# Split weights kept in DRAM, queries split at the projection, constants loaded one stage earlier, and 32-row scan blocks copied by ScalarE

## The chip, the cores and the metric

The kernel runs on one core of a Trainium2 chip. The metric is the device time of one execution in microseconds. The core has a matrix engine (PE, with its weight loads shown as PEld), a vector engine (DVE), an activation engine (ACT), a general engine (POOL), a queue engine (SP) that does nothing but issue transfers, and 16 DMA engines that carry the transfers of all queues. Each engine runs its own instruction list strictly in order; semaphores make one wait for another. An instruction that waits therefore holds everything behind it on its engine, and for SP that means every transfer behind a waiting one.

## What is computed

Two layers of an encoder over 2048 tokens of width 1024. Each layer normalises its input, multiplies it with one wide input matrix, feeds three head groups (A: gated linear attention, B: softmax attention with the difference of two maps, C: a gated recurrence), gates each group, multiplies with an output matrix, normalises and adds:

```python
for layer in range(2):
    h = rms_norm(x, norm_pre[layer])
    proj = h @ w_in[layer]                       # 1024 x 4128
    (gq, gk, gv, gg, gaf, gab, dq, dk, dv, dg, hq, hzf, hzb, hi, hg) = split(proj)
    y_a = gla_branch(gq, gk, gv, gg, ...)        # two scans, forward and backward
    y_b = diff_branch(dq, dk, dv, dg, ...)       # rope(q), rope(k), softmax(q1 k1) - lam softmax(q2 k2)
    y_c = hgrn_branch(hq, hzf, hzb, hi, hg, lb)  # f = lb + (1-lb) sigmoid(z); two scans
    x = x + rms_norm(concat(y_a, y_b, y_c) @ w_out[layer], norm_post[layer])
```

Accuracy is kept by splitting a float32 number into a rounded high part and the rest: a product of two split matrices is three matrix products (high by high, high by low, low by high).

## The kernel before, in words

Each layer has four stages. **Part 0** projects tokens 0 to 1023, block by block: 16 blocks of 256 (once 288) columns of the input matrix. **Part 1** projects tokens 1024 to 2047 with the same 16 blocks, and between the projection's matmuls the scans of groups A and C are worked off. **Attention** sweeps 64 units (4 heads by 16 query blocks), and the **output stage** multiplies, normalises and adds. The blocks come in the order of two lists in the code: values, gates, keys and queries of A and C first, then values of B, two blocks of keys (`do_qk(..., "k", ...)`), two blocks of queries (`do_qk(..., "q", ...)`) and three blocks of gates.

A block's weights come through `wload_into`: in two halves POOL's queue loads raw float32 (`wraw`, one buffer), DVE casts the high part (`whi`), and the rest (`wlo`) is subtracted by POOL in part 0 and by DVE in part 1. `whi` and `wlo` have two buffers, so that the next block's weights are made while this block is multiplied. Part 1 loads and splits every block's weights again.

`do_qk` works in groups of 512 tokens, two in each part: 48 matmuls fill two PSUM banks, DVE makes four products with a table of cosines and sines (`cs`, one buffer, loaded for each group by SP), POOL adds them into `ru`. A key is then split (`rh` cast by ACT, `ru` minus `rh` by POOL) and stored to `dr_k`; a query is stored whole to `dr_q`. Keys and queries of four heads lie 32 rows each in DRAM, so that one store of 128 rows by 512 columns has the outer sizes 4 and 32:

```python
nc.sync.dma_start(dr_q[hc, half, :, sl], u)   # hc: 4 of 8 heads, 32 rows each
```

In attention `load_q` brings the queries of two blocks back in four transfers, and POOL splits them. `layer_constants` loads two small sets of vectors and a small matrix at the start of a layer, in the middle of the first blocks. `do_hz` makes the gates of group C: DVE copies the projection out of PSUM, ACT and DVE work out the logarithm and exponentials, and POOL (part 0) or DVE (part 1) scales by `oml`. In the scans, `put` moves the blocks of levels 3 to 6 out of PSUM by a masked copy on DVE (L613), and those of level 7 by two plain copies of 64 rows on ACT.

PSUM has eight banks. In part 0 the projection may use all eight; in part 1 it has four, and the scans have the other four. The order of instructions on each engine is set when the program is built, by a scheduler with a model of costs; on the chip it is fixed. The small working tiles of the projection (`ru`, `rz`, `rh`, `z`, `lse`, `lsm`, `vs`, ...) share one set of seven buffers (tag `t`), and a tile that is stored is held until its store has landed.

Of the kernel before, what the change touches and what calls it, by code (L numbers as in the profile page):

```python
# [11 lines left out]
F32 = mybir.dt.float32  # L12
# [9 lines left out]
P = 128  # L22
# [38 lines left out]
def tile_hybrid_encoder(  # L61
# [40 lines left out]
    dr_q = dram.tile([8, 2, 32, L], F32, name="dr_q")  # L102
# [8 lines left out]
    dr_x = dram.tile([L, D], F32, name="dr_x")  # L111
    dr_u = dram.tile([P, 16, 512], F32, name="dr_u")
# [95 lines left out]
    def wload_into(wp, l, eng, c0, n, halves=False):  # L208
        hi = wp.tile([P, KC, WN], F32R, tag="whi", name="whi")
        lo = wp.tile([P, KC, WN], F32R, tag="wlo", name="wlo")  # L210
        for q in range(2):
# [3 lines left out]
            if halves:  # L215
                for hf in range(2):
                    src = raw[:, :, :n].rearrange("p k (h s i) -> p k h s i", s=2, i=32)[:, :, :, hf]
                    dh = hi[:, ks, P * hf:P * hf + P].rearrange("p k (h i) -> p k h i", i=32)
                    dl = lo[:, ks, P * hf:P * hf + P].rearrange("p k (h i) -> p k h i", i=32)
                    nc.vector.tensor_copy(dh, src)  # L220
                    eng.tensor_tensor(dl, src, dh.bitcast(F32), op=ALU.subtract)
            else:
                nc.vector.tensor_copy(hi[:, ks, :n], raw[:, :, :n])
                eng.tensor_tensor(lo[:, ks, :n], raw[:, :, :n], hi[:, ks, :n].bitcast(F32), op=ALU.subtract)  # L224
# [14 lines left out]

    for l in range(DEPTH):  # L240
# [6 lines left out]
        ls = lay.tile([P, 2], F32, tag="ls", name="ls")  # L247
        neglam = lay.tile([P, 1], F32, tag="neglam", name="neglam")
        wa2 = lay.tile([96, 2, P], F32R, tag="wa2", name="wa2")
        ba = lay.tile([P, 2], F32, tag="ba", name="ba")  # L250
# [5 lines left out]
        with ExitStack() as s1:  # L256
# [11 lines left out]
            def layer_constants():  # L268
                lv = ev.tile([P, 512], F32, tag="t", name="lv").rearrange("p (a n) -> p a n", n=64)
                lp = ev.tile([P, 512], F32, tag="t", name="lp").rearrange("p (a n) -> p a n", n=64)[:, :2]  # L270
                for i, a in enumerate((diff_lq1, diff_lk1, diff_lq2, diff_lk2)):
                    nc.sync.dma_start(lv[:, i], a[l:l + 1].to_broadcast([P, 64]))
                for i in range(2):
                    nc.vector.tensor_tensor(lp[:, i], lv[:, 2 * i], lv[:, 2 * i + 1], op=ALU.mult)
                nc.vector.reduce_sum(ls, lp, axis=AX.X)
                nc.scalar.activation(ls, ls, AF.Exp)
                nc.vector.tensor_tensor(neglam, ls[:, 1:2], ls[:, 0:1], op=ALU.subtract)
                nc.vector.tensor_scalar(neglam, neglam, -lam_init, None, op0=ALU.add)

                wraw = ev.tile([96, 512], F32, tag="t", name="wa").rearrange("p (d n) -> p d n", d=4)[:, :2]  # L280
                nc.vector.memset(wraw, 0.0)
                for d, (wa, b) in enumerate(((gla_wa2_fwd, gla_ba_fwd), (gla_wa2_bwd, gla_ba_bwd))):
                    for i in range(3):
                        nc.sync.dma_start(wraw[32 * i + 16 * d:32 * i + 16 * d + 16, d], wa[l])
                    nc.sync.dma_start(ba[:, d:d + 1], b[l].unsqueeze(1))
                nc.vector.tensor_copy(wa2, wraw)
                nc.vector.tensor_tensor(wa2[64:96], wraw[64:96], wa2[64:96].bitcast(F32), op=ALU.subtract)
# [36 lines left out]
            def do_qk(c0, cb, which, part):  # L324
                hc = slice(4 * cb, 4 * cb + 4)
                w = wload(c0 + 256 * cb, 256, part, halves=True)
                for g in (2 * part, 2 * part + 1):
# [5 lines left out]
                    for half, (a, b, op) in enumerate(((p1, p2, ALU.subtract), (p2, p1, ALU.add))):  # L333
# [4 lines left out]
                        nc.gpsimd.tensor_tensor(u, u, z, op=op)  # L338
                        if which == "q":
                            nc.sync.dma_start(dr_q[hc, half, :, sl], u)  # L340
                        else:
                            rh = ev.tile([P, 512], F32R, tag="t", name="rh")
                            nc.scalar.copy(rh, u)
                            nc.gpsimd.tensor_tensor(u, u, rh.bitcast(F32), op=ALU.subtract)
# [6 lines left out]
            def do_vs(c0, dst, dst0, part, w=None):  # L351
                w = w or wload(c0, 256, part)
# [81 lines left out]
            def do_hz(c0, d, part):  # L434
                w = wload(c0, 256, part)
                for m in range(2):
                    for g in (2 * part, 2 * part + 1):
                        ps = mm_ch(w, m * P, g)
                        sl = slice(g * 512, (g + 1) * 512)
                        z = ev.tile([P, 512], F32, tag="t", name="zh")  # L440
                        nc.vector.tensor_copy(z, ps)
                        e, lm = log_sig(z)
                        f = ev.tile([P, 512], F32, tag="t", name="f")
                        nc.scalar.activation(f, lm, AF.Exp)
                        he = nc.gpsimd if part == 0 else nc.vector
                        he.tensor_scalar(f, f, oml[:, l, m:m + 1], lb[:, l, m:m + 1], op0=ALU.mult, op1=ALU.add)
                        he.tensor_scalar(f, f, F_FLOOR, None, op0=ALU.max)
                        nc.sync.dma_start(dr_fh[d, m, :, sl], f)
                        kk = ev.tile([P, 512], F32, tag="t", name="kk")
                        nc.vector.scalar_tensor_tensor(e, z, 0.0, e, op0=ALU.max, op1=ALU.add)  # L450
                        nc.scalar.activation(kk, e, AF.Exp, scale=-1.0)
                        he.tensor_scalar(kk, kk, oml[:, l, m:m + 1], None, op0=ALU.mult)
# [27 lines left out]
            for i, b in enumerate(first + rest):  # L480
                b(0)
                if i == 0:
# [7 lines left out]
                    layer_constants()  # L490
# [9 lines left out]
            def scan_group(ti, g, tot):  # L500
# [91 lines left out]
                for lev in range(1, 8):  # L592
# [6 lines left out]
                    else:  # L599
# [5 lines left out]
                        def put(a, ps, j, lev=lev):  # L605
# [529 lines left out]
```

## Time and profile before

| | |
|---|---|
| median of 3 runs | 3637.28 us (3628.71 to 3641.9) |
| the profiled execution | 3641.44 us, of it span 3639.6 us |
| PE busy | 3513.4 us, 97% |
| DVE, ACT, POOL busy | 2560.3, 1927.8, 1459.6 us |
| DMA | 430.49 MB, mean 118 GB/s |

The profile is of one execution, whose time lies 0.1% above the median. "Busy" counts the time in which an engine had an instruction under way. Matmuls overlap one another, so PE counts as busy also where it runs slower than it could; a stretch of PE at the lower of its two clock levels (1.2 and 2.4 GHz) counts as busy too, and shows in the granted clock. Layer 0 takes about the first 1828 us and layer 1 the rest; the stages of layer 0 lie at 0 to 395 (part 0), 395 to 1003 (part 1, scans until about 920), 1003 to 1630 (attention) and 1630 to 1828 us (output).

### The profile page before, as it was taken

To read this page: it belongs to the slowest core of one execution; us is meant where nothing else is said; L and a number is where in the kernel's file an instruction comes from. 1 tells how busy PE (TensorE), PEld (TensorE's weight loads), DVE (VectorE), ACT (ScalarE), POOL (GpSimd) and SP (SyncE) were. 2 spreads that over 40 slices of the span, in tenths; PEclk is the share of its full clock that TensorE was granted. 3 is DMA by queue.
4 is the path that set the end of the run, shared out by engine and by line. 5 is a ranking of instruction groups with operands and counts; after the bars stand their busy time and mean duration, and the time that the engine had idled before them with its cause. 6 is when DMAs were issued, how large, how long until landed. Compare 5 with 4: busy or idle time off the path is not lost.

```text
span 3639.6 us, 62254 instructions
## 1 busy us (share of the span) xinstructions
PE 3513.4 (97%) x23296; PEld 3159.5 (87%) x23296; DVE 2560.3 (70%) x4426; ACT 1927.8 (53%) x4340; POOL 1459.6 (40%) x1454
## 2 busy tenths in 40 slices
PE   8999999998989999999989999999999899999999
PEld 7898988987978999888878989889878799999887
DVE  5422699987389999985324227999863899999733
ACT  4520455542377888874225215555423778888722
POOL 4545410012476667720035454100125867767100
PEclk9999999998999999999999999999989999999999
DMA  4444544544441333213334444445444413322143
GB/s 155 127 139 134 151 128 139 157 126 139 136 133 34 120 109 97 73 43 132 120 109 128 140 136 139 140 145 154 133 123 141 125 42 120 118 83 73 34 139 116
DMA packets 293645, 430.49 MB, mean 118 GB/s; under 512 B 42400, under 2 KB 185312, under 8 KB 291040
## 3 DMA queue, kind: packets, MB, share of 16 engines
q1 hardware_dynamic: 268896, 333.71, 29.7%
q0 software_dynamic: 22336, 90.71, 8.4%
q8 instruction: 184, 3.01, 0.3%
q10 hardware_dynamic: 2112, 2.10, 0.2%
q14 instruction: 117, 0.96, 0.1%
HBM read 275.82 MB, written 152.57 MB: 118 GB/s over the span
## 4 chain that ended last, share of the span: by engine, by line
PE 67%; DVE 13%; DMA 10%; POOL 4%; issue 3%; ACT 1%; SPq 1%; DVEq 0%; POOLq 0%; ACTq 0%
PE pp L306 14%; PE pp L297 12%; PE pob L1045 10%; PE po L938 9%; PE s L875 5%; PE s L876 5%; PE pt L927 5%; DMA wraw<-in_w_in_dram 3%; DVE mx L880 3%; DMA cs<-c_rope 2%; PE pm L587 2%; DVE e L921 2%; PE pm L568 1%; DMA ust<-dr_u 1%; PE poi L825 1%
## 5 line engine op out<-in xcount | busy, mean ns | idle before, releaser
L880 DVE TENSOR_REDUCE mx<-s 128x1 f32<-128x1024 f32 x512 | 623.1, 1217 | 54.3 <-PE s L876 52.9
L889 ACT ACTIVATE e<-s,mx 128x1024 f32<-128x1024 f32 x512 | 571.7, 1121 | 74.8 <-DVE mx L880 53.3
L306 PE MATMUL pp<-wlo,hhi 128*128 128x256 f32 (+1 forms) x2048 | 589.1, 288 | 7.1 <-POOL wlo L224 6.8
L306 PE MATMUL pp<-whi,hhi 128*128 128x256 f32 (+1 forms) x2048 | 585.2, 286 | 5.5 <-DVE ru L335 4.5
L306 PE MATMUL pp<-whi,hlo 128*128 128x256 f32 (+1 forms) x2048 | 588.4, 287 | 0.5 <-DVE hlo L195 0.5
L938 PEld LDWEIGHTS po<-vt,wt 128*128 128x128 f32 x4096 | 537.6, 192 | 47.9 <-ACT o L945 5.8
L938 PE MATMUL po<-vt,wt 128*128 128x128 f32 x4096 | 544.0, 276 | 1.6 <-ACT o L945 1.6
L875 PE MATMUL s<-ks,aqh 128*128 128x512 f32 x1024 | 452.4, 442 | 19.8 <-ACT e L889 15.1
L214 POOL DMA_DIRECT2D wraw<-in_w_in_dram x124 | 96.0, 774 | 920.4 <-DVE wlo L224 348.6
L876 PE MATMUL s<-ks,aql 128*128 128x512 f32 x1024 | 407.2, 398 | 14.2 <-POOL aql L732 14.1
L297 PE MATMUL pp<-hhi,whi 128*128 128x512 f32 x1024 | 412.5, 403 | 0.0
L297 PE MATMUL pp<-hlo,whi 128*128 128x512 f32 x1024 | 411.2, 402 | 0.0
L297 PE MATMUL pp<-hhi,wlo 128*128 128x512 f32 x1024 | 409.0, 399 | 0.0
L306 PEld LDWEIGHTS pp<-wlo,hhi 128*128 128x128 f32 x2048 | 390.0, 190 | 10.5 <-POOL wlo L224 7.6
L306 PEld LDWEIGHTS pp<-whi,hhi 128*128 128x128 f32 x2048 | 391.9, 191 | 8.0 <-issue 4.8
L921 DVE SCALAR_TENSOR_TENSOR e<-e,gam 128x1024 f32<-128x1024 f32 x256 | 392.3, 1533 | 0.0
L306 PEld LDWEIGHTS pp<-whi,hlo 128*128 128x128 f32 x2048 | 390.5, 191 | 1.8 <-DVE hlo L195 0.7
L931 ACT COPY wt<-pt 128x512 f32<-128x512 f32 x512 | 301.3, 589 | 118.9 <-PE pt L927 115.7
L927 PE MATMUL pt<-ident,e 128*128 128x128 f32 x2048 | 310.1, 274 | 1.2 <-ACT wt L931 0.6
L927 PEld LDWEIGHTS pt<-ident,e 128*128 128x128 f32 x2048 | 241.9, 142 | 2.9 <-ACT wt L931 1.2
L875 PEld LDWEIGHTS s<-ks,aqh 128*128 128x128 f32 x1024 | 196.4, 192 | 51.7 <-ACT e L889 23.3
L297 PEld LDWEIGHTS pp<-hhi,whi 128*128 128x128 f32 x1024 | 194.6, 190 | 45.0 <-issue 0.9
(190 smaller groups left out, 7042.9 us busy)
## 6 DMA issues: line engine op xcount, KB each, us to landing
wraw<-in_w_in_dram POOLq DMA_DIRECT2D x116, 512.0 KB, 4.8
cs<-c_rope SPq DMA_DIRECT2D x32, 512.0 KB
dr_gate<-z SPq DMA_DIRECT2D x64, 256.0 KB
aq<-dr_q SPq DMA_DIRECT2D x256, 64.0 KB
ks<-dr_k POOLq DMA_DIRECT2D x16, 1024.0 KB, 8.0
y<-dr_y SPq DMA_DIRECT2D x32, 512.0 KB
dr_qs<-qt SPq DMA_DIRECT2D x48, 256.0 KB
qs<-dr_qs SPq DMA_DIRECT2D x24, 512.0 KB
```

The lines of the kernel that those rows point to most:

```text
L214: nc.gpsimd.dma_start(raw[:, :, :n], w_in[l].rearrange("(k p) c -> p k c", p=P)[:, ks, c0:c0 + n])
L297: nc.tensor.matmul(ps.rearrange("p (a t) -> p a t", t=P), w[a][:, k, c:c + P], b[g][:, :, k], start=n == 0, stop=n == 3 * KC - 1)
L306: nc.tensor.matmul(ps, b[g][:, t % 4, k], w[a][:, k, :n], start=cnt == 0, stop=cnt == 3 * KC - 1)
L875: nc.tensor.matmul(s[:, i], self.qh[:, c, js], kk, start=True, stop=False)
L876: nc.tensor.matmul(s[:, i], self.ql[:, c, js], kk, start=False, stop=True)
L880: nc.vector.tensor_reduce(mx[:, k:k + 1], self.s[k].rearrange("p a n -> p (a n)"), axis=AX.X, op=ALU.max, negate=True)
L889: nc.scalar.activation(self.es[c][:, n * 1024:(n + 1) * 1024], self.s[kk].rearrange("p a n -> p (a n)"), AF.Exp, bias=self.mx[:, m:m + 1], ...
L921: nc.vector.scalar_tensor_tensor(es[0][:, hs], es[1][:, hs], gm[:, 8 + n:9 + n], es[0][:, hs], op0=ALU.mult, op1=ALU.add)
L927: nc.tensor.transpose(pt[:, i], self.es[0][:, (4 * q + i) * P:(4 * q + i + 1) * P], ident)
L931: nc.scalar.copy(wt, self.pt[q])
L938: nc.tensor.matmul(self.po, self.wt[q][:, i], self.v[:, k], start=k == 0, stop=k == NT - 1)
L1045: nc.tensor.matmul(pos[:, n], a[:, k], b[k][:, n * 512:(n + 1) * 512], start=cnt == 0, stop=cnt == 3 * KC - 1)
```

## The change

Four edits. (1) The split weights of part 0 are stored to DRAM (`dr_w`, by SP) and part 1 loads them ready made (`w_again`, POOL's queue, twice the bytes of the raw weights), with no cast and no subtraction. (2) A query is split in `do_qk` like a key, and each half is stored twice, in the layout in which attention wants it: eight stores for a group of 512 tokens instead of two. `load_q` is two transfers and no arithmetic. (3) `layer_constants` of layer 1 is issued at the start of layer 0's output stage. (4) In the scans the blocks of level 6 (32 rows by 32 columns) leave PSUM by four plain copies on ACT instead of one masked copy on DVE; and `do_hz` reads PSUM directly, with its scalings on ACT.

```diff
-    dr_q = dram.tile([8, 2, 32, L], F32, name="dr_q")
+    dr_q = dram.tile([8, 2, 2, 2, 32, L], F32, name="dr_q")
+    dr_w = dram.tile([17, 2, P, KC * WN], F32, name="dr_w")
...
+    def w_save(w, c0, n):
+        i = w_at.setdefault(c0, len(w_at))
+        for j in range(2):
+            nc.sync.dma_start(dr_w[i, j, :, :KC * n].rearrange("p (k c) -> p k c", c=n), w[j].bitcast(F32))
+    def w_again(wp, c0, n):
+        w = w_tiles(wp, n)
+        for j in range(2):
+            nc.gpsimd.dma_start(w[j].bitcast(F32), dr_w[w_at[c0], j, :, :KC * n].rearrange("p (k c) -> p k c", c=n))
+        return w
...
             def wload(c0, n, part, halves=False):
-                return wload_into(wp, l, nc.gpsimd if part == 0 else nc.vector, c0, n, halves)
+                return w_again(wp, c0, n) if part else wload_into(wp, l, c0, n, halves)
...
+                        rh = ev.tile([P, 512], F32R, tag="t", name="rh")
+                        nc.scalar.copy(rh, u)
+                        nc.gpsimd.tensor_tensor(u, u, rh.bitcast(F32), op=ALU.subtract)
                         if which == "q":
-                            nc.sync.dma_start(dr_q[hc, half, :, sl], u)
+                            for dup in range(2):
+                                nc.sync.dma_start(dr_q[hc, 0, half, dup, :, sl], rh.bitcast(F32))
+                                nc.sync.dma_start(dr_q[hc, 1, half, dup, :, sl], u)
...
-                        z = ev.tile([P, 512], F32, tag="t", name="zh")
-                        nc.vector.tensor_copy(z, ps)
-                        e, lm = log_sig(z)
+                        e, lm = log_sig(ps)
...
-                            if lev == 7:
-                                r0, r1 = slice(64 * j, 64 * j + 64), slice(64 - 64 * j, 128 - 64 * j)
-                                nc.scalar.copy(a[r0, ..., 64:128], ps[r0, ..., 64:128])
-                                nc.scalar.copy(a[r1, ..., 0:64], ps[r1, ..., 0:64])
+                            if lev >= 6:
+                                for r in range(0, P, h):
+                                    b = ((P - h - r if j else r) // h ^ 1) * h
+                                    nc.scalar.copy(a[r:r + h, ..., b:b + h], ps[r:r + h, ..., b:b + h])
...
             def load_q(h, qp):
-                qr = ak.tile([P, 2, 256], F32, tag="aq", name="aq", bufs=2)
-                for half in range(2):
-                    for s in range(2):
-                        p0 = 64 * half + 32 * s
-                        nc.sync.dma_start(qr[p0:p0 + 32], dr_q[2 * h:2 * h + 2, half, :, qp * 256:(qp + 1) * 256].rearrange("c p t -> p c t"))
-                nc.gpsimd.tensor_copy(qh, qr)
-                nc.gpsimd.tensor_tensor(ql, qr, qh.bitcast(F32), op=ALU.subtract)
+                for i, q in enumerate((qh, ql)):
+                    nc.sync.dma_start(q.bitcast(F32), dr_q[2 * h:2 * h + 2, i, :, :, :, qp * 256:(qp + 1) * 256]
+                                      .rearrange("c a d p t -> (a d p) c t"))
...
                 w_st, w_first = open_w(l + 1)
                 ep = s2.enter_context(tc.tile_pool(name=f"ep{l}", bufs=EPB, side="left"))
+                consts = layer_tiles()
+                layer_constants(l + 1, ep, *consts)
```

The order of instructions shows at three places. The first is SP's list in part 0 where the key blocks end and the query blocks begin (each row one instruction, `x2` two alike in a row; `dr_k` and `dr_q` are stores, `cs` is the load of the table). Before:

```order
L345 DMA dr_k<-rh 4x32x512
L346 DMA dr_k<-ru 4x32x512
L330 DMA cs<-c_rope 128x2x512
L340 DMA dr_q<-ru 4x32x512 x2
L330 DMA cs<-c_rope 128x2x512
L340 DMA dr_q<-ru 4x32x512 x2
```

At the same place in the changed program, from the first query store on:

```order
L371 DMA dr_q<-rh 4x32x512 x2
L357 DMA cs<-c_rope 128x2x512
L372 DMA dr_q<-ru 4x32x512 x2
L371 DMA dr_q<-rh 4x32x512 x2
L372 DMA dr_q<-ru 4x32x512 x2
L371 DMA dr_q<-rh 4x32x512 x2
L357 DMA cs<-c_rope 128x2x512
L372 DMA dr_q<-ru 4x32x512 x2
L219 DMA dr_w<-whi 128x2048
L371 DMA dr_q<-rh 4x32x512 x2
L219 DMA dr_w<-wlo 128x2048
```

Between one load of `cs` and the next there now stand eight stores of queries instead of two, and every second time two saves of weights.

The second place is DVE's list in part 0 at the last query group, where the casts of the second gate block's weights stand among the products with `cs`. Before:

```order
L223 CAST whi<-wraw 128x4x256
L337 TENSOR_TENSOR rz<-pp,cs 128x512
L335 TENSOR_TENSOR ru<-pp,cs 128x512
L337 TENSOR_TENSOR rz<-pp,cs 128x512
L393 COPY z<-pp 128x512
L321 SCALAR_TENSOR_TENSOR lsm<-z,lse 128x512
L223 CAST whi<-wraw 128x4x256
```

And in the changed program:

```order
L241 CAST whi<-wraw 128x1024
L362 TENSOR_TENSOR ru<-pp,cs 128x512
L364 TENSOR_TENSOR rz<-pp,cs 128x512
L362 TENSOR_TENSOR ru<-pp,cs 128x512
L364 TENSOR_TENSOR rz<-pp,cs 128x512
L241 CAST whi<-wraw 128x1024
L424 COPY z<-pp 128x512
```

In both the second cast of the second gate block stands behind the last group's products; nothing lets it pass them.

The third place is SP's list in part 1, at the end of the scans (`dr_u` and `dr_oi` are the scans' last stores, `aq` and, in the changed program, `aqh` and `aql` are attention's first loads of queries). Before:

```order
L330 DMA cs<-c_rope 128x2x512
L340 DMA dr_q<-ru 4x32x512 x2
L662 DMA dr_oi<-oi 128x4x128
L699 DMA dr_u<-ut 64x3x128
L699 DMA dr_u<-ut 64x4x128
L728 DMA aq<-dr_q 32x2x256 x3
L340 DMA dr_q<-ru 4x32x512
L330 DMA cs<-c_rope 128x2x512
```

In the changed program:

```order
L374 DMA dr_k<-rh 4x32x512
L375 DMA dr_k<-ru 4x32x512
L755 DMA aqh<-dr_q 128x2x256
L755 DMA aql<-dr_q 128x2x256
L758 DMA aga<-dr_gate 128x2x128
L755 DMA aqh<-dr_q 128x2x256
L755 DMA aql<-dr_q 128x2x256
L758 DMA aga<-dr_gate 128x2x128 x2
L371 DMA dr_q<-rh 4x32x512 x2
L357 DMA cs<-c_rope 128x2x512
L372 DMA dr_q<-ru 4x32x512 x2
```

Attention's first loads, whose tiles take the scans' memory, now stand ahead of all four query groups of part 1; before, they stood in the middle of them.

## Rows read from the trace of the kernel before

**Rows 1.** The page: span, busy time, and one row of the DMA queues (packets, MB, share).

```profile
span 3639.6 us, 62254 instructions
PE 3513.4 (97%) x23296; PEld 3159.5 (87%) x23296; DVE 2560.3 (70%) x4426; ACT 1927.8 (53%) x4340; POOL 1459.6 (40%) x1454
...
q1 hardware_dynamic: 268896, 333.71, 29.7%
```

**Rows 2.** Busy time by stage, layer 0 and the start of layer 1.

```profile
core 0: us, PE busy (x) PEld busy (x) DVE busy (x) ACT busy (x) POOL busy (x), PEclk, DMA share, GB/s
0.00:50.00 50.00, 32.15 (x252) 31.27 (x253) 34.73 (x63) 24.39 (x69) 17.42 (x16) 1.00 0.61 199
...
0.00:395.00 395.00, 372.70 (x2340) 337.00 (x2341) 155.57 (x244) 136.08 (x282) 201.12 (x150) 0.99 0.44 138
395.00:905.00 510.00, 489.70 (x3437) 438.59 (x3437) 446.13 (x814) 236.89 (x510) 73.25 (x62) 0.97 0.48 140
1003.00:1150.00 147.00, 134.98 (x850) 118.50 (x851) 131.94 (x225) 107.28 (x243) 112.19 (x100) 0.93 0.34 92
...
1828.00:1900.00 72.00, 60.59 (x425) 57.18 (x424) 17.93 (x33) 18.16 (x40) 28.78 (x20) 0.91 0.35 104
```

**Rows 3.** Two stretches in which stores alone moved; columns as in rows 2.

```profile
160.00:163.00 3.00, 3.00 (x14) 2.44 (x13) 1.02 (x1) 1.54 (x4) 2.37 (x2) 1.00 0.97 370
...
286.00:298.00 12.00, 12.00 (x53) 9.74 (x52) 3.16 (x6) 0.62 (x1) 5.89 (x6) 1.00 0.27 104
```

**Rows 4.** The chain that ended last, key and query blocks of part 0: start, us, what.

```profile
245.79 13.94 PE pp L297 x61
259.75 11.82 DMA dr_k<-ru
...
272.31 6.35 DMA cs<-c_rope
...
297.96 8.14 DMA cs<-c_rope
...
308.74 7.60 DMA cs<-c_rope
...
322.70 9.32 DMA wraw<-in_w_in_dram
...
359.40 2.36 POOL wlo L224
```

**Rows 5.** DVE in order of time, the last product of the last query group.

```profile
345.44 0.68 DVE L337 TENSOR_TENSOR rz<-pp,cs 128x512 f32<-128x512 f32 x1
```

**Rows 6.** The same chain at the end of part 1.

```profile
917.39 3.58 DMA dr_u<-ut
...
923.11 13.86 DMA cs<-c_rope
...
939.92 57.55 PE pp L306 x480
```

**Rows 7.** Groups of instructions from 395 to 905: line, operation, count | busy, mean ns | idle before.

```profile
L613 DVE COPY_PREDICATED att<-masks,pm 128x512 f32<-128x512 uint8 x128 | 87.2, 733 | 1.6 <-PE pm L587 1.4
...
L224 DVE TENSOR_TENSOR wlo<-wraw,whi 128x1024 fp32r<-128x1024 f32 (+1 forms) x18 | 22.8, 1269 | 0.0
...
L223 DVE CAST whi<-wraw 128x1024 fp32r<-128x1024 f32 (+1 forms) x18 | 12.7, 706 | 7.9 <-DMA wraw<-in_w_in_dram 4.2 <-PE pp L297 2.6 <-PE pp L306 1.0
L221 DVE TENSOR_TENSOR wlo<-wraw,whi 128x512 fp32r<-128x512 f32 x16 | 11.0, 729 | 0.0
...
L220 DVE CAST whi<-wraw 128x512 fp32r<-128x512 f32 x16 | 6.1, 427 | 7.5 <-DMA wraw<-in_w_in_dram 5.5 <-PE pp L306 2.0
```

**Rows 8.** The same view of ACT.

```profile
L608 ACT COPY att<-pm 64x256 f32<-64x256 f32 x32 | 11.7, 366 | 37.4 <-DVE att L613 26.4 <-PE pm L587 5.9 <-DVE nt L625 4.2
```

**Rows 9.** PE's groups that waited, 1828 to 1900 us.

```profile
L414 PE MATMUL ppa<-ident,low 128*32 128x128 f32 x8 | 2.3, 355 | 11.4 <-ACT low L390 11.4
```

**Rows 10.** PE's groups that waited, 1003 to 1150 us.

```profile
L876 PE MATMUL s<-ks,aql 128*128 128x512 f32 x115 | 48.6, 422 | 7.1 <-POOL aql L732 7.1
```

More of the change, by code (lines that the diff above doesn't have):

```diff
@@ L206, in prenorm_load, with w_tiles, wload_into @@
         return halves
-    def wload_into(wp, l, eng, c0, n, halves=False):
-        hi = wp.tile([P, KC, WN], F32R, tag="whi", name="whi")
-        lo = wp.tile([P, KC, WN], F32R, tag="wlo", name="wlo")
+    w_at = {}
+    def w_tiles(wp, n):
+        return [wp.tile([P, KC * WN], F32R, tag=name, name=name)[:, :KC * n].rearrange("p (k c) -> p k c", c=n)
+                for name in ("whi", "wlo")]
+    def w_save(w, c0, n):
[7 more added lines that the diff above has]
+        return w
+    def wload_into(wp, l, c0, n, halves=False):
+        hi, lo = w_tiles(wp, n)
         for q in range(2):
@@ L220, in wload_into @@
                     nc.vector.tensor_copy(dh, src)
-                    eng.tensor_tensor(dl, src, dh.bitcast(F32), op=ALU.subtract)
+                    nc.gpsimd.tensor_tensor(dl, src, dh.bitcast(F32), op=ALU.subtract)
             else:
-                nc.vector.tensor_copy(hi[:, ks, :n], raw[:, :, :n])
-                eng.tensor_tensor(lo[:, ks, :n], raw[:, :, :n], hi[:, ks, :n].bitcast(F32), op=ALU.subtract)
+                nc.vector.tensor_copy(hi[:, ks], raw[:, :, :n])
+                nc.gpsimd.tensor_tensor(lo[:, ks], raw[:, :, :n], hi[:, ks].bitcast(F32), op=ALU.subtract)
+        w_save((hi, lo), c0, n)
         return hi, lo
@@ L246, in tile_hybrid_encoder @@
         tots = [lay.tile([P, 2, 16], F32, tag=f"tot_{ti}", name=f"tot_{ti}") for ti in range(3)]
[L247 to L250, printed above, removed]
+        if l == 0:
+            neglam, wa2, ba = consts = layer_tiles()
+        else:
+            neglam, wa2, ba = consts
         if l == 0:
@@ L439, in do_hz @@
                         sl = slice(g * 512, (g + 1) * 512)
[L440 to L442 removed]
+                        e, lm = log_sig(ps)
                         f = ev.tile([P, 512], F32, tag="t", name="f")
                         nc.scalar.activation(f, lm, AF.Exp)
[L445 to L447 removed]
+                        nc.scalar.activation(f, f, AF.Copy, scale=oml[:, l, m:m + 1])
+                        nc.vector.tensor_scalar(f, f, lb[:, l, m:m + 1], F_FLOOR, op0=ALU.add, op1=ALU.max)
                         nc.sync.dma_start(dr_fh[d, m, :, sl], f)
                         kk = ev.tile([P, 512], F32, tag="t", name="kk")
[L450 removed]
+                        nc.vector.scalar_tensor_tensor(e, ps, 0.0, e, op0=ALU.max, op1=ALU.add)
                         nc.scalar.activation(kk, e, AF.Exp, scale=-1.0)
[L452 removed]
+                        nc.scalar.activation(kk, kk, AF.Copy, scale=oml[:, l, m:m + 1])
                         nc.sync.dma_start(dr_kh[d, m, :, sl], kk)
```

54 lines of the change are left out of this document (30 added, 24 removed).

## The prediction

> **What bounds the kernel now.** I read the page first: PE is busy for 3513.4 of 3639.6 us, DVE for 2560.3 [rows 1]. That leaves 126 us in which PE stood still, so the busy time by stage comes next, to see where that is [rows 2]. Part 0 has 22.3 us, 17.9 of them in the first 50, the scans from 395 to 905 have 20.3 us with DVE busy 446 of 510, attention's first 147 us have 12.0, and the start of layer 1 has 11.4 of 72 us. Beside the idle time stands the granted clock: 0.97 in the scans is another 15 us of 510 at full speed, 0.93 at the start of attention 10 us of 147, 0.91 at the start of layer 1 6.5 us of 72. So this is a kernel on PE's path almost everywhere; an edit off that path can give back some 20 to 35 us in a layer, and an edit that makes PE wait costs its full wait.
>
> The third view is the chain in the last blocks of part 0 [rows 4]. It does not run through PE there but through transfers: a store of `dr_k` that takes 11.82 us, loads of `cs` that take 6 to 8 us, a weight load of 9.32 us. PE stays busy in it only because eight PSUM banks let it run four groups ahead. That made me look at what the stores do to the DMA engines [rows 3]. From 160 to 163 us stores of 128 by 512 move alone, at a share of 0.97 of the 16 engines and 370 GB/s. From 286 to 298 us the stores of `dr_k`, of the same bytes but with outer sizes 4 and 32, move alone, at a share of 0.27 and 104 GB/s. 0.27 of 16 is 4.3 engines: a store of this form keeps four engines busy and leaves twelve idle. One store of 262,144 bytes then takes 2.5 us, against 0.71 us at 370 GB/s.
>
> The row does not say why it is four. The Trainium skill, "DMA: Bandwidth & Descriptors", section "Why a DMA increments its semaphore by 16 and not by 1", says that a transfer is spread over the largest number of engines up to 16 that divides the slowest dimension of both of its sides; by it the outer size 4 sets four engines, and the changed query stores, whose outer size is 4 as well, get four too. By that rule 2.5 us holds for them; if the row had another cause they might take 0.71 us, which is the first rival.
>
> **A check on four engines.** Those four also carry a sixteenth each of everything else, and SP's transfers pass in order. A key group has four stores (10.1 us), its `cs` (524,288 bytes at 370 GB/s, 1.4) and half a block's raw weights (1.4): 12.9 us. In the chain `cs` was issued at 272.31 and, three groups later, at 308.74: 12.1 us a group [rows 4]. PE's 48 matmuls take 11.0 us (61 in 13.94). The key blocks run at the pace of these four engines already. A query group before, with two stores, comes to 7.8 us and let them recover.
>
> **The change, part by part.**
>
> *Query stores and saves in part 0.* A query group now has eight stores: 20.2 us, with `cs` and weights 23.0 against 11.0 on PE. A save of a block's split weights is 2,097,152 bytes at 370 GB/s: 5.7 us on every engine. By SP's list I follow the loads of `cs`, since DVE's products wait for them. Before, the four loads for the query groups landed at 306.1 and 316.3 [rows 4] and then until DVE ended the last product at 346.1 [rows 5]. After: two saves stand ahead of the first (306.1 + 11.4 = 317.5); a third and two query stores ahead of the second (316.3 + 11.4 + 5.7 + 5.0 = 338.4); 23.0 more for the third (361.4); 23.0 and the save of a gate block for the fourth (390.1). With some 3 us of products DVE is through at 393 instead of 346. The second cast of the second gate block's weights stands behind it in DVE's list, so cast (0.7) and subtraction (2.36) end at 396. Before, that subtraction ended at 361.8 and PE went on [rows 4]. PE starts this block 34 us later; the first gate block and its banks are no help, since it is done by then. PE at rest for so long loses its clock for a while: 3 us, half of what the start of layer 1 shows for a shorter rest. **37 us a layer, 74 in all.** From below: the four engines are over PE's pace by 4 x (25.9 - 11.0) = 60 us (25.9 with half a save), and four groups of PSUM, 44 us, may hide all but 16. From above: 24 more stores that lose 0.7 us each to other traffic, 52.
>
> *Queries at the end of part 1.* Here the weights come ready made on POOL's queue and no cast stands in DVE's list, so PE waits for PSUM alone. But attention's first loads stand ahead of the query stores in SP's list, and they cannot go before the scans give their memory back. Before, that was at 921 (917.39 + 3.58), the last `cs` was issued at 923.11, landed at 937, and PE was dense from 939.92 [rows 6]. I let the scans end 30 us sooner (bounds 10 and 45; the next term says why): at 891. Two stores and `cs` later it is 898, then two groups of 24.4 (with twice the weight bytes): 947, and products until 950. PE is dense 10 us later than before; query tiles held by their stores, which the gates need, add 2. **12 us a layer, 24 in all**, bounds -15 and +30.
>
> *What DVE loses in the scans.* Of 446 us: casts and subtractions 22.8 + 12.7 + 11.0 + 6.1 = 52.6 us, and a quarter of the masked copies, 32 x 0.733 = 23.5 us [rows 7], 76 us together; what `do_hz` gives comes on top, unpriced. The waits of DVE for raw weights go as well. PE lost 20.3 us and some clock in this stretch; I give it half, 10 us, and 20 us more because in PE's list the scans' last products stand some 120 projection matmuls earlier (27 us at 13.94 / 61 each, less where they are the narrow ones). These are the 30 us above; they end in the wait for query stores, and are not counted again. The four small copies on ACT are 128 a layer, at most 0.37 us each (a copy of twice the columns [rows 8]), 47 us; ACT has 273 us free there. Without that cover it would cost these 47.
>
> *Early constants.* PE waits 11.4 us at the start of layer 1 for a chain that begins with these loads [rows 9]; the stretch lost 6.5 us to the clock too. **-12**, bounds -17 and -5. In the output stage they lie beside dense PE work; if DVE stuck there on them, most of the 12 would come back.
>
> *Queries ready for attention.* PE waited 7.1 us for POOL's low part in the first 147 us [rows 10], with 10 us of clock. **-14 for both layers**, bounds -35 and 0. Later POOL's work was hidden anyway.
>
> *First save and early traffic:* **+2**, beside transfers of the first tokens; bounds 0 and 6.
>
> Sum: 74 + 24 - 12 - 14 + 2 = +74 on the profiled 3641, 3715; the median lies 4 us lower, so **3711 us**, 2.0% slower.
>
> The Trainium skill, the same page, section "Queues, rings and completion order", says that each engine goes round between the queues that have work. By it POOL's weight loads pass SP's pile-up; the trace has 9.32 us for one at such a time [rows 4], late but not stuck. If they stood in one line, part 1 would pay some 20 us more a layer.
>
> **The rivals.**
>
> *The query stores stay hidden.* If they spread over 16 engines, eight take 5.7 us, a group 5.7 + 1.4 + 1.4 + 2.9 = 11.4 against PE's 11.0, and nothing piles up. Then part 0 pays some 5 us a layer for saves, part 1 gains 15, and the sum is 10 - 30 - 12 - 14 + 2 = -44: 3593. For it: twelve engines are idle in rows 3. Against it: the same shape runs on four. It decides at about 0.7 us a store.
>
> *Every save is exposed.* If weight loads and stores slow in all 16 blocks and half of each save's 5.7 us reaches PE, 32 x 2.9 = 91 comes on top: 3802. Against it: after its first 50 us part 0 lost only 4.4 us of PE, so weights come in time there; the DMA share is 0.44 [rows 2], and a save adds 5.7 of a block's 22 us, about a quarter.
>
> *Gain and loss cancel.* PSUM and the idle engines hide half: part 0 pays 20 a layer, part 1 gains 5: 40 - 10 - 24 = +6, about 3643.
>
> **Numbers.** A measurement of this kernel tells 0.5%, 18 us, from no change. Forecast 0.57, stores hidden 0.15, saves exposed 0.12, cancelled 0.11, and 0.05 for a worse wait that I do not see. Slower 0.57 + 0.12 + 0.05 = 0.74, same 0.11, faster 0.15. The forecast's own range is 3660 to 3765: the bounds of part 0 alone give -42 and +30, those of part 1 -54 and +36, and both ends together are unlikely. For 8 in 10 I take 3615 to 3790, which holds the cancelled case and most of the exposed saves.
>
> **What would show it.** Right: PE idle for some 25 us or more near 370 in layer 0, its waits ending on `wlo`; loads of `cs` in the chain at over 20 us; query stores with a DMA share near 0.27 for long stretches. Wrong: `cs` landing in under 12 us between query groups; a share well above 0.5 during query stores; PE waiting for `whi` or `wlo` in the value blocks too (the saves); part 0 ending near 395. The scans should show DVE at some 360 us, and the start of layer 1 no wait for `low`.

## The result, and the profile after

The changed kernel takes 3836.49 us (median of 4 runs, 3828.99 to 3851.3) against 3635.64 for the kernel before, run beside it: a ratio of 1.0558, 95% interval 1.052 to 1.0596. That is slower, as forecast, but by 200 us where the forecast had 74, and outside its range of 3615 to 3790. It is the case to which the forecast gave 0.05, a worse wait that it did not see. The profiled execution took 3833.43 us, span 3831.7, so the two profiles lie 192 us apart.

The page of the changed kernel, in the lines that answer to [rows 1]:

```profile
span 3831.7 us, 62186 instructions
PE 3523.0 (92%) x23296; PEld 3170.8 (83%) x23296; DVE 2313.1 (60%) x4154; ACT 2045.2 (53%) x4692; POOL 1284.3 (34%) x1310
...
q1 hardware_dynamic: 305120, 443.29, 35.3%
```

PE stands still for 309 us instead of 126, although DVE, the engine that was relieved, is busy for 247 us less.

The stages of all kernels below were cut at the same instructions (last projection matmul of a part, first output matmul), in us of the profiled execution. By this cut part 0 of the kernel before ends at 407 us and part 1 at 997, not at the rougher 395 and 1003 used above.

| kernel | layer 0: part 0, part 1, attention, output | layer 1 | span |
|---|---|---|---|
| before | 407, 590, 634, 197 | 392, 590, 632, 198 | 3640 |
| changed | 482, 631, 621, 199 | 447, 630, 624, 198 | 3832 |

Part 0 lost 75 and 55 us, part 1 41 and 39; attention gave back 12 and 8. The difference of 20 between the two parts 0 lies in their first quarter: counted from the layer's first projection matmul, PE comes to the gates behind the query blocks 13 us late in layer 0 and 9 us early in layer 1. From there to the end of part 0 it is 138 us instead of 77 in layer 0, and in both layers together 125 more than before.

The busy time by stage after, columns as in [rows 2]: part 0, the scans, the start of attention, the start of layer 1, and two pieces of the stretches in question.

```profile
0.00:482.00 482.00, 396.37 (x2444) 356.01 (x2445) 146.88 (x247) 154.09 (x314) 183.21 (x138) 0.92 0.58 201
482.00:992.00 510.00, 481.87 (x3402) 431.10 (x3401) 361.52 (x683) 276.91 (x651) 60.44 (x61) 0.97 0.54 175
1112.00:1259.00 147.00, 133.11 (x881) 118.29 (x880) 134.96 (x237) 114.19 (x254) 104.10 (x89) 0.97 0.41 115
1933.00:2005.00 72.00, 69.75 (x473) 65.47 (x472) 15.26 (x26) 19.43 (x41) 30.74 (x21) 0.98 0.57 201
400.00:410.00 10.00, 0.80 (x2) 0.50 (x2) 2.49 (x4) 1.23 (x2) 7.28 (x5) 0.50 0.26 102
975.00:985.00 10.00, 5.29 (x21) 3.49 (x19) 0.00 (x0) 0.00 (x0) 0.67 (x2) 0.83 1.04 365
```

The last row but one is the signature of [rows 3] again: query stores alone, a share of 0.26, 102 GB/s, while PE has 0.8 us of work in 10. At those rates a store of 262,144 bytes takes 2.6 us.

DVE in order of time in part 0, where the queries end and the gates begin (start, us, instruction, and in brackets the idle time before it and its releaser):

```profile
370.72 0.69 DVE L362 TENSOR_TENSOR ru<-pp,cs 128x512 f32<-128x512 f32 x1 [14.63 <-DMA cs<-c_rope]
...
398.62 0.69 DVE L362 TENSOR_TENSOR ru<-pp,cs 128x512 f32<-128x512 f32 x1 [21.63 <-DMA cs<-c_rope]
...
403.74 0.69 DVE L364 TENSOR_TENSOR rz<-pp,cs 128x512 f32<-128x512 f32 x1 [3.23 <-DMA dr_q<-ru]
404.35 0.68 DVE L241 CAST whi<-wraw 128x1024 fp32r<-128x1024 f32 x1
408.90 0.69 DVE L424 COPY z<-pp 128x512 f32<-128x512 f32 x1 [3.87 <-DMA dr_q<-rh]
...
426.84 0.69 DVE L348 SCALAR_TENSOR_TENSOR lsm<-z,lse 128x512 f32<-128x512 f32 x1 [6.87 <-DMA dr_q<-ru]
431.96 0.69 DVE L424 COPY z<-pp 128x512 f32<-128x512 f32 x1 [4.43 <-DMA dr_q<-rh]
...
443.01 0.69 DVE L241 CAST whi<-wraw 128x1024 fp32r<-128x1024 f32 x1
...
455.84 0.69 DVE L241 CAST whi<-wraw 128x1024 fp32r<-128x1024 f32 x1 [7.56 <-DMA wraw<-in_w_in_dram]
```

Two things are to be seen. Up to 404 DVE waits for the table `cs`, as forecast. After 404 the queries are done on DVE, and it waits on: each of the next four copies of a gate block (two are shown) waits for the landing of a query store, and the first cast of the third gate block's weights stands behind those copies until 443. The second, at 455.84, then waits for its raw weights. PE's waits between 395 and 482 end on the three casts shown and on the subtractions behind them (us in total, times, longest):

```profile
PE pp L333 <- DVE whi L241: 38.0, 3, 21.1
...
PE pp L333 <- POOL wlo L242: 9.2, 3, 4.6
```

Part 1's end is an SP list. SP in order of time; the second number is how long the issue itself took:

```profile
965.30 0.36 SPq L755 DMA_DIRECT2D aqh<-dr_q  x1
...
968.68 8.00 SPq L758 DMA_DIRECT2D aga<-dr_gate  x2
976.78 7.22 SPq L371 DMA_DIRECT2D dr_q<-rh  x2
984.10 1.99 SPq L357 DMA_DIRECT2D cs<-c_rope  x1
...
1002.44 4.43 SPq L357 DMA_DIRECT2D cs<-c_rope  x1
...
1031.34 2.37 SPq L357 DMA_DIRECT2D cs<-c_rope  x1
...
1063.68 3.37 SPq L372 DMA_DIRECT2D dr_q<-ru  x2
```

And the answers to [rows 7 to 10], the masked copies and the new small copies from 482 to 992, then the two places whose waits were to go:

```profile
L641 DVE COPY_PREDICATED att<-masks,pm 128x512 f32<-128x512 uint8 x96 | 65.4, 735 | 17.3 <-PE pm L615 17.2
```

```profile
L637 ACT COPY att<-pm 32x128 f32<-32x128 f32 (+1 forms) x192 | 56.2, 293 | 12.6 <-PE pm L615 7.5 <-DVE att L641 2.0 <-DVE nt L653 0.4
```

```profile
L445 PE MATMUL ppa<-ident,low 128*32 128x128 f32 x8 | 1.2, 272 | 0.0
```

```profile
L899 PE MATMUL s<-ks,aqh 128*128 128x512 f32 x121 | 54.3, 449 | 12.3 <-DMA aqh<-dr_q 5.8 <-ACT e L913 5.8 <-DVE z L424 0.8
L900 PE MATMUL s<-ks,aql 128*128 128x512 f32 x120 | 48.6, 405 | 0.2 <-DMA aql<-dr_q 0.2
```

Both waits are gone (11.4 and 7.1 us before), but at the start of attention 5.8 us of waiting for the load of the queries' high part have come in place of the 7.1. DVE, which waited 1.6 us for PE at the masked copies in [rows 7], now waits 17.3; its load from 482 to 992 is 361.5 us, as forecast, and part 1 is no shorter for it in the end.

### The profile page after: what moved, and what is told of

Its sections match the earlier page's. It is cut to its first block, busy times and chain, and to the rows that moved or that the text cites. A ratio compares the mean times of both kernels' runs of the same rounds, so it can differ in the third digit from the quotient of the medians.

```text
span 3831.7 us, 62186 instructions
## 1 busy us (share of the span) xinstructions
PE 3523.0 (92%) x23296; PEld 3170.8 (83%) x23296; DVE 2313.1 (60%) x4154; ACT 2045.2 (53%) x4692; POOL 1284.3 (34%) x1310
## 5 line engine op out<-in xcount | busy, mean ns | idle before, releaser
L333 PE MATMUL pp<-whi,hhi 128*128 128x256 f32 (+1 forms) x2048 | 602.0, 294 | 151.5 <-DVE whi L241 98.0
L333 PE MATMUL pp<-wlo,hhi 128*128 128x256 f32 (+1 forms) x2048 | 599.6, 293 | 23.9 <-POOL wlo L242 23.8
L333 PE MATMUL pp<-whi,hlo 128*128 128x256 f32 (+1 forms) x2048 | 598.8, 292 | 0.5 <-DVE hlo L196 0.5
L333 PEld LDWEIGHTS pp<-whi,hhi 128*128 128x128 f32 x2048 | 404.0, 197 | 156.4 <-DVE whi L241 79.0
L333 PEld LDWEIGHTS pp<-wlo,hhi 128*128 128x128 f32 x2048 | 403.3, 197 | 28.1 <-POOL wlo L242 26.9
L333 PEld LDWEIGHTS pp<-whi,hlo 128*128 128x128 f32 x2048 | 404.6, 198 | 1.9 <-DVE hlo L196 0.9
L945 DVE SCALAR_TENSOR_TENSOR e<-e,gam 128x1024 f32<-128x1024 f32 x256 | 346.6, 1355 | 0.0
L367 ACT CAST rh<-ru 128x512 fp32r<-128x512 f32 x64 | 39.7, 620 | 496.9 <-POOL ru L365 443.7
L362 DVE TENSOR_TENSOR ru<-pp,cs 128x512 f32<-128x512 f32 x64 | 43.9, 686 | 357.9 <-DMA cs<-c_rope 337.4
```

What stands on the lines that cost most here:

```text
L333: nc.tensor.matmul(ps, b[g][:, t % 4, k], w[a][:, k, :n], start=cnt == 0, stop=cnt == 3 * KC - 1)
L362: nc.vector.tensor_tensor(u, a, cs[:, 0], op=ALU.mult)
L945: nc.vector.scalar_tensor_tensor(es[0][:, hs], es[1][:, hs], gm[:, 8 + n:9 + n], es[0][:, hs], op0=ALU.mult, op1=ALU.add)
```

## The experiments

Theory F: the loss comes from the form of the query stores, which keeps four DMA engines busy. Rivals: N, the number of stores and of held tiles; S, the saves of weights. Where nothing else is said a time is of a single run; the kernel before, run beside them, had medians of 3633 to 3643 us. Four runs of the changed kernel lie within 22 us and seven of the kernel before within 11, so a difference of that size between two single runs tells nothing by itself.

**1. The form alone** (3658.6 us).

```diff
-    dr_q = dram.tile([8, 2, 2, 2, 32, L], F32, name="dr_q")
+    dr_q = dram.tile([2, 2, 2, 2, P, L], F32, name="dr_q")
...
-    nc.sync.dma_start(dr_q[hc, 0, half, dup, :, sl], rh.bitcast(F32))   # 4x32x512
+    nc.sync.dma_start(dr_q[cb, 0, half, dup, :, sl], rh.bitcast(F32))   # 128x512
```

> The changed kernel with one thing other: the four heads of a query store lie as one run of 128 rows in DRAM, so the same eight stores of the same bytes have the outer size 128 instead of 4 and 32 (attention then loads its queries in eight pieces of 32 rows instead of two of 128). Theory F (the query stores are slow because their form keeps four DMA engines busy): a store takes some 0.7 us instead of 2.5, PE's four stops in part 0 (12 + 26 + 13 + 9 us a layer) and the 45 us at the end of part 1 go, part 0 of layer 0 ends near 420 instead of 482, and the time is 3600 (3570 to 3650). Rival N (eight stores and two held tiles each are too many whatever their form): part 0 still ends beyond 465, over 3790. Rival S (the saves of the split weights are the load): over 3780.

The same eight stores of the same bytes, and 175 of the 192 us are gone (span 3656.8); part 0 takes 429 and 394 us, part 1 594 and 599. N and S fall as main causes, though the time lies just above the range that I gave for F: what is left over is no gain, as experiment 3 shows. In this kernel's trace, a stretch of query stores, table, weights and saves, columns as in [rows 2]:

```profile
355.00:372.00 17.00, 16.18 (x113) 16.19 (x114) 5.66 (x9) 1.39 (x3) 12.27 (x10) 0.80 1.02 371
```

A share of 1.02 and 371 GB/s: all 16 engines. The rows also tell fewer engines from slower ones. In the two stretches of [rows 3] an engine is busy for about as long with 2,048 bytes, one row of a store: 0.27 of 16 engines over 104 GB/s make 85 ns, 0.97 of 16 over 370 GB/s make 86 (an estimate from these rows). A slow store is not slower on its engine; fewer engines carry it.

The Trainium skill, "DMA: Bandwidth & Descriptors", section "Why a DMA increments its semaphore by 16 and not by 1", has the rule by which 128 rows spread over 16 engines and an outer size of 4 over four; by that rule the run had to come out so, and the trace agrees.

**2. Half the stores, in the slow form** (3679.59 us): each half stored once, `dr_q[hc, 0, half, :, sl]`, and read twice by attention.

> The changed kernel with each half of a query stored once instead of twice, in the same form of outer sizes 4 and 32 (attention then reads each stored row twice, in eight pieces): four stores a group instead of eight. If the loss begins only where the four engines fall behind PE by more than PSUM covers (theory F with a threshold): four stores 10.1, table 1.4, weights 1.4 and half a save 2.9 make 15.8 us a group against 11.0 on PE, 19 us over in four groups, within the cover of PSUM: 3665 (3645 to 3695), nearly all of the 175 us that the form of 128 rows gave back. If the loss is in proportion to the stores: half of the 175, 3745.

Span 3677.8, 21 us above the run with 128 rows. Half the slow stores cost 21 us, hardly more than single runs differ, and all of them 175. So the loss is no fixed price per store. That it begins where the four engines fall behind PE is what I expected (3665), and the run lies in that range.

**3. The parts of the change by themselves.** The changed kernel without edit 2 (3657.7 us):

> The changed kernel without its second edit: queries are stored whole, two stores a group, and split by POOL in attention as before; saves, early constants and scan copies stay. Theory F: the loss was all in the query stores, so what is left is the gain of the other edits and the late start of layer 0 (+12): 3600 (3570 to 3640). Rival S (the saves): PE still waits for weights behind the query blocks, 3740 or more. Rival N gives the same as F here.

The kernel before with edit 2 alone (3761.61 us):

> The kernel before with the second edit alone: eight query stores of outer sizes 4 and 32 a group, no saves. Theory F and rival N: part 0 loses some 50 to 60 us a layer and part 1 60 to 70, attention gives 10 back: 3840 (3780 to 3880), as slow as the whole change or slower, since the shorter scans are missing. Rival S: within 1% of before, 3600 to 3670.

The kernel before with edit 1 alone (3653.47 us):

> The kernel before with the first edit alone: split weights saved in part 0 and loaded ready made in part 1. Theory F: the saves pass beside the matmuls; layer 0 starts some 12 us late, the scans lose casts and subtractions on DVE and end 10 to 20 us sooner a layer: 3620 (3590 to 3650). Rival S: 3740 or more, with PE waiting for weights in the value and gate blocks.

The kernel before with edit 4 alone (3648.61 us):

> The kernel before with the fourth edit alone: blocks of 32 rows copied by ACT, gates of group C read from PSUM. Theory D (DVE bounds the scans, what it is relieved of comes back): part 1 is shorter by 10 us a layer, 3610 (3600 to 3625). Theory L (the scans go at the pace of a chain from engine to engine; DVE had slack, and four small copies in a row lengthen a step): part 1 the same or longer by up to 10 us a layer, 3634 to 3655.

The changed kernel without edit 1 (3748.32 us):

> The changed kernel without its first edit: every block's weights are loaded and split in both parts, nothing is saved; query stores, early constants and scan copies as changed. The saves alone cost the kernel before 20 us, the query split alone 128 us, the whole change 200. Theory I (saves and slow stores make each other worse, since the saves stand in SP's list between the stores and add their bytes to the same four engines): 3765 (3745 to 3790), so that the saves cost some 65 us here. Rival A (the costs only add up, and the rest is the scan copies): 3815 (3805 to 3830).

| kernel | layer 0: part 0, part 1, attention, output | layer 1 | span |
|---|---|---|---|
| before | 407, 590, 634, 197 | 392, 590, 632, 198 | 3640 |
| changed, queries whole | 426, 594, 633, 198 | 389, 585, 633, 198 | 3656 |
| before + query split | 443, 620, 623, 197 | 430, 626, 623, 198 | 3760 |
| before + saves | 425, 581, 632, 197 | 403, 584, 632, 198 | 3652 |
| before + scan copies | 410, 597, 630, 197 | 396, 585, 633, 198 | 3647 |
| changed, no saves | 444, 622, 623, 198 | 419, 620, 623, 198 | 3747 |

Without edit 2 no gain is left over: my 3600 was 58 us too low, since the relief of DVE in the scans brings nothing that can be told (part 1 moves by +4 and -6 there, by +7 and -5 with the scan copies alone; theory L, not D). With the saves alone part 1 is 9 and 6 us shorter, but one kernel run twice (3562.56 us and the profiled run of the same kernel below) already differs by 3 and 5 us there. Two more expectations failed: I had the query split alone at 3840, as slow as the whole change, and the saves alone at 3620. The query split alone costs 120 us in the spans and the saves alone 12, so that both would add up to 132 (scan copies add 7, early constants take some 10 away); the whole change costs 192. Taking the saves out of the changed kernel gives 85 us (theory I; 65 expected): 38 and 28 in the two parts 0, 8 and 10 in the two parts 1. Saves cost little by themselves and much beside slow stores.

**4. Saves on POOL's queue** (3822.96 us): `nc.gpsimd.dma_start(dr_w[...])` instead of `nc.sync`.

> The changed kernel with the saves issued on POOL's queue instead of SP's. The bytes are the same, but the saves no longer stand in SP's list: no store, table or constant waits behind a save that waits for its cast. Theory W (part of the cost is SP waiting): layer 0 starts some 10 us sooner, and each layer's query blocks gain 5 to 15 us: 3800 (3780 to 3815). Rival T (only the traffic counts): 3815 to 3835, if anything from the start of layer 0.

The time lies in the range of rival T. Part 0 of layer 0 is 7 us shorter, part 0 of layer 1 3 us longer, and part 1 3 and 2 us shorter: SP's waiting behind saves is at most a small part. What is left, that the bytes are the larger one, is argued and not shown.

**5. The tail behind the last table.** What was still unexplained, the second pair of PE's stops, I first put down to working tiles that query stores hold. Eight tiles (3832.2 us; for the room, the gates' norm weights then have one buffer instead of two) and six (3840.4), by `EVB`, with the slow stores:

> The changed kernel with eight working tiles instead of seven (and one buffer instead of two for the gates' norm weights, to make room). Theory H (the missing cost is tiles held by query stores that have not landed): one tile more is one store pair of some 5 us less to wait at the end of each query stretch, four stretches: 3815 (3800 to 3825). Rival C (all of it is the late table, the tiles don't matter): 3828 to 3840.

> The changed kernel with six working tiles. Theory H: 5 us more at each of four stretches, and in the control with fast stores next to nothing: 3855 (3845 to 3885). Rival C: 3830 to 3842.

The same two with 128 rows (3643.3 and 3659.73 us):

> Control for eight tiles: the changed kernel with query stores in the form of 128 rows, and eight working tiles. Theory H: the stores land soon, so a tile more gives little: 3655 (3645 to 3660). If tiles are short in general, as much as with the slow stores: 3640.

> Control for six tiles: the changed kernel with query stores in the form of 128 rows, and six working tiles. Theory H: 3660 (3655 to 3668). If tiles are short in general: 3680 or more, as much as with the slow stores.

Spans 3830, 3832 and 3839 with eight, seven and six tiles: theory H in this form falls. If anything the eighth tile gave more with the fast stores (15 us, about as much as single runs differ). DVE with eight tiles:

```profile
399.52 0.68 DVE L364 TENSOR_TENSOR rz<-pp,cs 128x512 f32<-128x512 f32 x1
400.12 0.79 DVE L241 CAST whi<-wraw 128x1024 fp32r<-128x1024 f32 x1
400.83 0.68 DVE L424 COPY z<-pp 128x512 f32<-128x512 f32 x1
413.76 0.69 DVE L348 SCALAR_TENSOR_TENSOR lsm<-z,lse 128x512 f32<-128x512 f32 x1 [12.26 <-DMA dr_q<-ru]
...
442.14 0.69 DVE L241 CAST whi<-wraw 128x1024 fp32r<-128x1024 f32 x1
```

The first copy starts 8 us sooner than with seven, the cast that PE waits for 0.9 us sooner. Next, the gates' stores out of SP's list (`nc.gpsimd.dma_start` for `dr_gate`), with seven tiles (3836.95 us) and eight (3842.48):

> The changed kernel with the gates' stores issued on POOL's queue, where their last multiplication runs, instead of SP's. Theory L (the gates wait in line: a gate's tile is held until its own store has passed all query stores in SP's list): the second pair of PE stops in part 0 and the last stops of part 1 shrink by half or more, 3785 (3760 to 3810). Theory E (the tiles are with the query stores until these land, in whatever order the gates' stores go): 3820 to 3840.

> The same with eight working tiles instead of seven, so that one more tile turns over among the gates while the query stores land. Theory L: 3770 (3745 to 3800), below the run with seven. Theory E: 3815 to 3840; if POOL's issue work (some 1 us for each of 32 stores a layer) stands in the way, more.

Theory E: the third cast stands at 443.9 and 441.2, and the time does not move. So neither the number of tiles nor the line on SP sets the tail, and DVE's longest waits in it end on the landings of query stores, or on ACT, which in the changed kernel waits 7.2 us for one itself. With 128 rows the same cast stands at 390.58, 15 us behind the first gate copy, where it is 34 us with the slow form. What is shown is that the tail goes with the slow form. That the pile has to drain on four engines before the gates run freely is the reading that is left; no view here shows the engines one by one.

**6. A better kernel.** The kernel before with its own key and query stores in 128 rows (3599.56 us; `dr_k[cb, half, 0, :, sl]`, keys read back in four pieces of 32 rows):

> The kernel before with its own key and query stores in the form of 128 rows (keys read back in four pieces of 32 rows). Theory F with a threshold: the four engines were at PE's pace here (12.9 against 11.0 us a group) and hidden by PSUM, so little is to be had: 3630 (3618 to 3640). If every such store cost PE time, the 24 stores a layer at 1.8 us less each would give up to 40 us a layer: 3560 to 3600.

With it the query split, stored once, and the early constants, without saves and scan copies (3562.56 us, where I expected 3605):

> The kernel before with queries split in the projection, but stored once and in the form of 128 rows (keys too), and with the early constants of layer 1; no saves, no scan copies. Attention gains some 9 us a layer (as in the runs with split queries), the start of layer 1 some 11: 3605 (3590 to 3625). If the split of queries is itself a burden in part 0 and part 1, whatever its stores (ACT's cast, POOL's subtraction, two tiles): 3635 or more.

The same kernel again, and once more with saves on POOL's queue, four runs of each:

> The same kernel as in the run of keys and queries in 128 rows, queries stored once and early constants, without saves and scan copies, now timed in rounds: 3562 (3550 to 3572), a ratio of 0.980 to the kernel before.

> The kernel of keys and queries in 128 rows, queries stored once, early constants, and beside it the saves of split weights on POOL's queue (loaded ready made in part 1). If the saves are worth what they gave part 1 alone (9 and 6 us a layer) once SP does not wait for them: 3550 (3535 to 3560). If their traffic costs as much as the casts: 3562 or more.

| kernel | layer 0: part 0, part 1, attention, output | layer 1 | time, ratio to before |
|---|---|---|---|
| before, 128 rows | 399, 571, 633, 197 | 385, 581, 633, 198 | 3599.56 |
| + split, constants | 399, 574, 620, 198 | 372, 578, 622, 198 | 3567.18, 0.9799 (0.9782 to 0.9815) |
| + saves by POOL | 409, 584, 621, 201 | 383, 583, 622, 198 | 3601.58, 0.9894 (0.9879 to 0.9909) |

The kernel before itself lost 34 us to the slow form (42 between the spans), more than I thought could be had, and most of it in part 1. The query split is worth having once its stores are fast: against the first row attention gains 13 and 12 us, and the other parts pay 3 us at most. The 13 us in part 0 of layer 1 go with the early constants. The gain over the kernel before, 1.9 to 2.2%, is clear of the noise. The saves cost 34 us there (the ratios' intervals lie apart) where I expected a gain, 3550.

## Why the prediction was right or wrong

**Right: the mechanism up to the second gate block.** A store of outer sizes 4 and 32 runs at 102 GB/s, the table waits behind such stores, DVE behind the table, the second gate block's weights behind DVE. The forecast had DVE through at 393; it was through at 404.4, of which 13 us had come in at the start of the layer. PE goes on in the second gate block at 410.5; without those 13 us that is 36 us later than before, where 34 were forecast. One piece lay elsewhere: 10.8 + 1.6 us of PE's waits, at 345, fell on the first gate block, which the forecast took as done by then, and 21.1 + 4.6, at 384, on the second.

**Wrong: where the pile ends (part 0, 37 forecast, 62 measured).** The step that failed is "PE starts this block 34 us later", with nothing after it. I followed the pile to the last load of the table. Behind that load stand the last group's eight stores, some 20 us, and a save, 5.7 by my own price. DVE's copies of the gates wait for these stores to land, and the third gate block's casts stand behind the copies: two more stops of 12.6 and 8.9 us, 21.5 that were not in the sum. Experiment 5 shows that they go with the form and not with the number of tiles or the line on SP.

**Nearly right in part 0, wrong in part 1: the saves' price.** In the value, key and early gate blocks they hide, as forecast (from the third block on PE, at 85.4, to the first gate matmul behind the queries, at 343.7, it is 258 us, before 254). Beside the slow stores they cost 25 us a layer in part 0. The sum had 11.4 + 5.7 + 5.7 = 22.8 for them, as time by which they move the table, and the run without saves bears that out; its last product of the queries:

```profile
373.20 0.69 DVE L345 TENSOR_TENSOR rz<-pp,cs 128x512 f32<-128x512 f32 x1 [2.59 <-DMA dr_q<-ru]
```

That is 18 us sooner than in the changed kernel, the late start taken off. Without the 22.8 the forecast of 37 would be some 14 for the query stores alone; the same stretch of part 0 takes 36 to 38 us more than before without any save. So it was the query stores' price that was too small, for the most part by the tail behind the last table. In part 1 the saves cost some 9 us, where the sum counted the ready-made weights as a gain. The rival "every save is exposed", with its 91 us, had nearly the right amount (85) by luck: not in all blocks, but beside the slow stores and at the start.

**Wrong: the start of layer 0 (+2 forecast, +13 measured).** DVE stood 15.86 us for the masks and cast them at 63.20; in the kernel before this wait was 9.21 and ended at 58.43. PE then waits 7.9 us in three stops up to 85.4, and from 80 to 90 its granted clock is 0.53. The run with saves alone has the wait too (16.82, 63.66), and the runs without saves do not start late. I put it down to SP's list, in which saves of the first blocks wait for their casts ahead of the masks and the layer's constants. Experiment 4 speaks against that: with the saves on POOL's queue the masks are cast at 66.31 and the third block starts at 85.2 all the same. Which part of a save costs this time stays open. Early constants: forecast -12, and PE's wait of 11.4 is gone.

**Wrong: part 1 (+12 forecast, +41 and +39 measured).** The scans did end sooner, 475 us after part 0 instead of 510, close to the 30 that I took. But I put this into the term as time, and it was mostly order. At the scans' last matmul 1562 of part 1's 2316 projection matmuls had begun, before it was 1683; and in the first 475 us of part 1 PE was busy for 458.6 us, before for 454.7. What the scans' products gained in PE's list, the projection behind them lost. Then the first table left SP 18.8 us after attention's first loads (965.30 to 984.10), and DVE's products with it began at 994.65, 29 us after these loads and not 7: attention's first keys, values and weights fill all engines at that moment (share 1.04). From there on the pace was as forecast (18.3 and 28.9 us between tables, 24.4 forecast), and the last group's stores came on top as in part 0. PE's five stops between 978 and 1076 are 42.8 us (14.0, 13.3, 8.2, 4.9 and 2.4).

**Right in the amount: attention.** -14 for both layers forecast, -20 measured, within its bounds; the query split alone gives as much (experiment 3). The wait for the low part is gone as forecast, but 5.8 us for loads have come in its place. In the first 147 us behind the last projection matmul PE stands still for 13.9 us, before for 14.7, at a granted clock of 0.97 instead of 0.93. Over the whole attention of layer 0 PE's idle time falls by 2.8 us and its busy time by 9.5: the waits that the forecast priced are the smaller part.

In numbers: query stretches of part 0 +125 (74 forecast), start of layer 0 +13 (2), the rest of layer 1's part 0 -9 (-12), part 1 +80 (24), attention -20 (-14), output +3; together 192.

## What to carry to other kernels

A store's outer size is a cost of its own: before adding transfers of a form, divide the GB/s of a stretch in which that form moves alone by that of a full one, and if a few engines carry it, change the layout first, here 34 us for the unchanged work and 175 for the changed. A pile of transfers ends with its last landing and not with the load that was waited for, so follow it to the last store and to whoever needs the tiles that it holds. Work taken from an engine that waits for others need not give anything back (247 us of DVE here), and that its stage's last instruction comes sooner may only be order.

## What the runs showed that I had not expected

Issues slow down to the pace of the pile. SP's issues of query stores in the kernel before (shortest, median and longest, ns):

```profile
L340 SPq DMA_DIRECT2D dr_q<-ru x32: 509/517/813, 309.4 to 2755.6; - x32
```

In the changed kernel the median is 2.4 us, about what such a store takes to move, and at the end of layer 1's part 1 the chain of the changed kernel runs through SP's issues alone from 2873.56 to 2941.92. Four of its pieces (start, us, what):

```profile
2905.11 2.43 SPq L372
2907.64 2.33 SPq L371
2910.02 2.47 SPq L371
2912.59 2.42 SPq L372
```

So a queue with such a pile holds back also what it carries for others, here the table and the attention's gates. And the slow form cost the kernel before 7 or 8 us a layer in part 0, where PE's waits at the gates were 4 us, and 19 and 9 in part 1. [rows 3] had shown the form, but what it cost only the run with the other layout showed.
